# A streaming encoder step on one core: GpSimd's two-tensor operations issued as pieces of at most 256 columns

## The chip, the core and the metric

The kernel runs on one core of a Trainium2 chip. The metric is the device time of one execution in microseconds (us); the time of a kernel is the median of several executions. Five engines take part: TensorE (PE in the profile; PEld are its weight loads), VectorE (DVE), ScalarE (ACT), GpSimd (POOL), and SyncE (SP), which issues the DMAs.

## What is computed

One inference step of a one-layer encoder, for 512 prompt frames with 16 meta tokens ahead of them (T columns) and 32 frames of a running stream. All arrays are float32.

```
x <- x + 1/2 * SwiGLU_1(RMSNorm(x))
h  = RMSNorm(x);  z = h @ W_in_all        # conv B, C, v | q latent | kv latent | rotary key | two gates
conv = W_conv_out(B * dwconv3_causal(C * v))
mla  = W_mla_out(chunk-causal latent attention, 16 heads, QK RMS norm)
x <- x + W_out_all(sigmoid(gate_conv) * conv + sigmoid(gate_mla) * mla)
x <- x + 1/2 * SwiGLU_2(RMSNorm(x))
```

The outputs are x of both groups and the caches for conv, kv latents and rotary keys. The model width is 1024, the FFN width 2816.

## The kernel before

Activations lie transposed: 128 features on the partitions, tokens on the columns (T = 560, or L = 544 without the meta tokens). To keep float32 precision, each operand of a matmul is held as two parts: `hi`, a cast by ScalarE, and `lo`, what the cast lost, a subtraction on VectorE or GpSimd. Each product is three matmuls (`mm3`, L136 to L139): hi*hi, hi*lo, lo*hi. The program is:

1. **First FFN** (`ffn`, L175). The gate and up projections go in pairs of column blocks, with a Strassen-like scheme on VectorE (`operands`, `combine`); the down projection follows in groups (`down`). At the end of each up job `up_job.finish` (L370) writes u into the pair `ah`/`al`; `al` is subtracted on GpSimd. As `down` ends, `done` (L613) calls `gained` (L476) per block of 128 features: GpSimd squares y (L484, L486) and adds it to the sum `sq` (L487); `token_rstd` (L489) then sums `sq` over the features on TensorE (L494).
2. **Mix stretch** (L655 on). Attention, head by head, is written in order, with `fill(us)` calls between its parts; `fill` (L881) draws from `stream` (L849), which has 48 blocks of plain projection matmuls (the conv, gate and conv-out columns, tile `f`). The next block's weights are loaded by `block` (L857) with `E=GP`, so their `lo` part `wl` is made by GpSimd. GpSimd also makes the conv taps' sums `cv` (L825), the products `b1` (L835, L836), and the squares `sqk` (L914) and `sqw` (L948) for the norms of K and Q. VectorE carries the norms' small chains (`rsqrt`, L144), K (L921, L925), Q (L959) and the softmax scaling `pw` (L1110).
3. **Merge.** For each of 8 blocks m, `gate` (L1204) loads a gate column block `sg`, multiplies it by R2 on GpSimd (L1207) and applies the sigmoid on ScalarE; `cb` is multiplied by it (L1217, GpSimd); after the `w_mla_out` product VectorE multiplies `sg` by it (L1220), GpSimd adds `cb` (L1221), and `split` (L1222) makes `mh`/`ml`. The `w_out_all` product of block m = 0 needs `mh` of all 8 blocks, in order of k.
4. **Second FFN**, as the first, and the output.

The subtraction's engine is chosen in `split`:

```
def split(hi, lo, src, E=None):
    a = S.copy(hi, src)
    return a, (E or V).tensor_sub(lo, src, f(hi))
...
block = lambda u: load([u[0]], E=GP)
...
split(ah[:, j], al[:, j], u[j], GP)
```

Weights arrive by SP's DMAs in `load` (L94): raw tile `wr` (2 buffers), `wh` and `wl` (3 buffers each). A framework draws the dependences from the columns that each instruction reads and writes, sets the semaphores, and orders each engine's instructions at build time with a model of their durations; on the chip each engine works its list in that fixed order.

Of the kernel before, what the change touches and what calls it, by code (L numbers as in the profile page):

```python
# [50 lines left out]
WMAX = KD * P  # L51


@with_exitstack
def encoder_step(ctx: ExitStack, tc: tile.TileContext, i, o):
    nc = tc.nc
    V, S, PE, GP = nc.vector, nc.scalar, nc.tensor, nc.gpsimd

    def dma(out, in_):
        return nc.sync.dma_start(out, in_)  # L60
# [454 lines left out]
    with ExitStack() as es:  # L515
# [15 lines left out]
        with tc.tile_pool(name="ps0", bufs=4, space=PSUM, reuse_waits="tile") as psum:  # L531
# [43 lines left out]
            for t, step in enumerate((3, 5, 8, 10, 6)):  # L575
                junk = pool.tile([P, D], F32, tag="tg", name="junk", bufs=2)
                src = xp[:, t] if t < 4 else xm[:MS]
                n = P if t < 4 else MS
# [54 lines left out]
        for ts in ((0, 1), (2, 3), (4,)):  # L633
            ps = acc()
            for k0, k1 in ((0, KD - 1), (KD - 1, KD)):
                for t in ts:
                    n = P if t < 4 else MS
# [6 lines left out]
            for t in ts:  # L644
                n = P if t < 4 else MS
# [9 lines left out]
    with ExitStack() as es:  # L655
# [423 lines left out]
        for h in range(HEADS):  # L1079
# [24 lines left out]
            n = NV[3] // 2  # L1104
# [36 lines left out]
            for j in range(NQ):  # L1141
                ps = bank("t")
                for t in range(j, NQ):
                    a = PO[t] + META + j * P
# [154 lines left out]
def build(inputs):  # L1299
    nc = bacc.Bacc("TRN2", target_bir_lowering=False, num_devices=1, dynamic_dma_scratch_size=1024)  # L1300
    arrays, ins = {}, {}
    for name, a in list(inputs.items()) + list(constants().items()):
        a = np.ascontiguousarray(a)
        arrays[f"in_{name}_dram"] = a
        ap = nc.dram_tensor(
            f"in_{name}_dram", a.shape, mybir.dt.from_np(a.dtype), kind="ExternalInput"
        ).ap()
        ins[name] = ap
    outs = [
        nc.dram_tensor(f"out_{n}_dram", s, F32, kind="ExternalOutput").ap()  # L1310
        for n, s in enumerate(_OUTS)
    ]
    with tile.TileContext(nc, schedule_with_timeline_sim=True) as tc:
        encoder_step(tc, ins, outs)
    return nc, arrays
# [6 lines left out]
```

## Time and profile before

| | |
|---|---|
| median of 3 executions | 1459.97 us (1458.66 to 1461.28) |
| profiled execution | 1461.02 us, its span 1459.1 us |
| TensorE busy | 1399.1 us (96%) |
| VectorE busy | 1055.0 us (72%) |
| ScalarE busy | 652.4 us (45%) |
| GpSimd busy | 381.8 us (26%), 283 instructions |
| mean granted TensorE clock | 0.989 of full speed |

Busy time is the time in which an engine had an instruction under way; matmuls overlap, so a busy TensorE may still be slowed. A line number such as L92 is that of the kernel before, and a helper's line stands for all its callers; the names behind it (`out<-in`) say which. FFN 1 ends near 416 us, the mix stretch lies between 432 and 956, the merge between 956 and 1064, FFN 2 after it.

### The profile page before, as it was taken

How to read it: one execution, taken by the hardware profiler on the slowest of the kernel's cores; microseconds unless marked ns; L12 is line 12 of the kernel's file. 1: busy time of each engine (PE TensorE's matmuls, PEld its weight loads, DVE VectorE, ACT ScalarE, POOL GpSimd, SP SyncE). 2: the span in 40 equal slices, each digit the busy share in tenths (PEclk: the TensorE clock that was granted, in tenths of full speed). 3: DMA queues.
4: the chain of work that ended last, by engine and by line, in shares of the span. 5: the costliest groups of instructions: out<-in, count | busy, mean ns of one | idle time of the engine just before them, and what ended most of it. 6: DMA issues, size and time to landing. Idle time of an engine off the chain costs nothing.

```text
span 1459.1 us, 26175 instructions
## 1 busy us (share of the span) xinstructions
PE 1399.1 (96%) x10667; PEld 1361.9 (93%) x10667; DVE 1055.0 (72%) x1703; ACT 652.4 (45%) x1220; POOL 381.8 (26%) x283
## 2 busy tenths in 40 slices
PE   6999999999999999899999999998989999999998
PEld 5899999999899998898899988998989999999998
DVE  5887878787676766966955958545797787978754
ACT  6543443435324354454554555543254353435341
POOL 0000001101474644444423322168410010001010
PEclk9999999999999999999999999998999999999999
DMA  6242323323343321222332224365433233324213
GB/s 169 65 126 71 116 73 102 91 84 87 90 119 90 97 73 57 79 63 60 102 90 78 82 90 151 117 190 158 133 92 97 73 116 88 115 60 130 70 44 94
DMA packets 215630, 141.59 MB, mean 97 GB/s; under 512 B 6415, under 2 KB 202914, under 8 KB 215510
## 3 DMA queue, kind: packets, MB, share of 16 engines
q1 hardware_dynamic: 215510, 139.93, 32.7%
q8 instruction: 83, 1.36, 0.4%
q14 instruction: 37, 0.30, 0.1%
HBM read 124.15 MB, written 15.76 MB: 96 GB/s over the span
## 4 chain that ended last, share of the span: by engine, by line
PE 75%; DVE 12%; issue 5%; POOL 4%; DMA 3%; ACT 2%; SPq 0%; DVEq 0%; POOLq 0%; ACTq 0%
PE b L137 9%; PE b L138 9%; PE b L139 9%; PE acc L137 7%; PE acc L138 7%; PE acc L139 7%; PE f L137 5%; PE f L138 4%; PE f L139 4%; DMA wr<-in_ffn_w_gate_dram 1%; POOL sg L1207 1%; PE late L137 1%; PE late L138 1%; PE late L139 1%; DVE pw L1110 1%
## 5 line engine op out<-in xcount | busy, mean ns | idle before, releaser
L91 ACT CAST wh<-wr 128x1024 fp32r<-128x1024 f32 (+2 forms) x165 | 166.7, 1018 | 238.6 <-PE acc L138 122.3
L137 PE MATMUL f<-xh,wh 128*128 128x272 f32 (+1 forms) x816 | 240.8, 295 | 4.2 <-DVE ext L815 2.1
L138 PE MATMUL f<-xl,wh 128*128 128x272 f32 (+1 forms) x816 | 239.6, 294 | 0.4 <-DVE xl L92 0.2
L139 PE MATMUL f<-xh,wl 128*128 128x272 f32 (+1 forms) x816 | 239.2, 293 | 0.0
L92 POOL TENSOR_TENSOR al<-tu,ah 128x560 fp32r<-128x560 f32 (+1 forms) x40 | 64.3, 1611 | 654.9 <-issue 392.2
L138 PE MATMUL acc<-al,wh 128*128 128x280 f32 (+1 forms) x704 | 203.8, 291 | 3.0 <-POOL al L92 3.0
L137 PE MATMUL acc<-ah,wh 128*128 128x280 f32 (+1 forms) x704 | 202.8, 291 | 1.7 <-ACT ah L91 1.0
L139 PE MATMUL acc<-ah,wl 128*128 128x280 f32 (+1 forms) x704 | 202.9, 291 | 0.0
L92 POOL TENSOR_TENSOR wl<-wr,wh 128x1024 fp32r<-128x1024 f32 (+1 forms) x50 | 119.9, 2399 | 211.2 <-ACT wh L91 191.4
L92 DVE TENSOR_TENSOR wl<-wr,wh 128x1024 fp32r<-128x1024 f32 (+2 forms) x115 | 153.2, 1338 | 24.1 <-ACT wh L91 20.3
L137 PEld LDWEIGHTS f<-xh,wh 128*128 128x128 f32 x816 | 155.2, 190 | 6.1 <-issue 2.3
L138 PEld LDWEIGHTS f<-xl,wh 128*128 128x128 f32 x816 | 155.5, 191 | 1.5 <-DVE xl L92 1.0
L139 PEld LDWEIGHTS f<-xh,wl 128*128 128x128 f32 x816 | 155.2, 190 | 0.3
L137 PE MATMUL b<-xsh,yh 128*128 128x280 f32 (+1 forms) x480 | 139.1, 290 | 0.8 <-ACT kept L319 0.6
L138 PE MATMUL b<-xsl,yh 128*128 128x280 f32 (+1 forms) x480 | 139.0, 290 | 0.0
L139 PE MATMUL b<-xsh,yl 128*128 128x280 f32 (+1 forms) x480 | 138.9, 289 | 0.1
L138 PEld LDWEIGHTS acc<-al,wh 128*128 128x128 f32 x704 | 132.5, 188 | 3.5 <-POOL al L92 3.5
L137 PEld LDWEIGHTS acc<-ah,wh 128*128 128x128 f32 x704 | 131.8, 188 | 2.7 <-ACT ah L91 1.4
L139 PEld LDWEIGHTS acc<-ah,wl 128*128 128x128 f32 x704 | 132.0, 188 | 0.2 <-DVE wl L92 0.2
L91 ACT CAST yh<-ws 128x1024 fp32r<-128x1024 f32 x80 | 84.0, 1049 | 90.1 <-PE b L138 82.3
L92 DVE TENSOR_TENSOR yl<-ws,yh 128x1024 fp32r<-128x1024 f32 x80 | 97.5, 1218 | 32.7 <-ACT yh L91 32.1
L407 DVE SCALAR_TENSOR_TENSOR tu<-acc,R 128x560 f32<-128x560 f32 (+1 forms) x80 | 58.1, 728 | 50.9 <-PE acc L139 50.8
(359 smaller groups left out, 3873.9 us busy)
## 6 DMA issues: line engine op xcount, KB each, us to landing
wr<-in_w_in_all_dram SPq DMA_DIRECT2D x43, 512.0 KB, 4.0
wr<-in_ffn_w_down_dram SPq DMA_DIRECT2D x32, 512.0 KB, 4.2
wr<-in_ffn_w_gate_dram SPq DMA_DIRECT2D x23, 512.0 KB, 3.9
wr<-in_ffn_w_up_dram SPq DMA_DIRECT2D x23, 512.0 KB, 5.1
wq<-in_ffn_w_gate_dram SPq DMA_DIRECT2D x20, 512.0 KB, 4.2
wq<-in_ffn_w_up_dram SPq DMA_DIRECT2D x20, 512.0 KB, 4.2
wr<-in_ffn_w_down_dram SPq DMA_DIRECT2D x16, 384.0 KB, 3.5
gt_dram<-b SPq DMA_DIRECT2D x16, 272.0 KB, 2.1
```

The lines of the kernel that those rows point to most:

```text
L91: a = S.copy(hi, src)
L92: return a, (E or V).tensor_sub(lo, src, f(hi))
L137: PE.matmul(out, a[0], b[0], start=start, stop=False, skip_group_check=onto)
L138: PE.matmul(out, a[0], b[1], start=False, stop=False, skip_group_check=onto)
L139: PE.matmul(out, a[1], b[0], start=False, stop=stop, skip_group_check=onto)
L407: V.scalar_tensor_tensor(t, ps[:, :, :n], 0.5, Rv, op0=ALU.mult, op1=ALU.mult)
L1110: V.tensor_scalar_mul(pv(t), pv(t), inv[:, t : t + 1])
L1207: GP.tensor_mul(sg, sg, R2[:, META:])
```

## The change

`GP`, which was `nc.gpsimd`, becomes a wrapper around it. Calls of tensor_add, tensor_sub and tensor_mul through it are cut along the first free dimension into equal pieces of at most 256 columns, each an instruction of its own; all other operations pass through. `make_identity` and the DMAs are not touched.

```
+class Pieces:
+    def __init__(self, engine):
+        self.engine = engine
+
+    def __getattr__(self, name):
+        op = getattr(self.engine, name)
+        if name not in ("tensor_add", "tensor_sub", "tensor_mul"):
+            return op
+
+        def pieces(out, a, b):
+            n = out.shape[1]
+            step = max(1, 256 // int(np.prod(out.shape[2:])))
+            count = -(-n // step)
+            cuts = [n * j // count for j in range(count + 1)]
+            for lo, hi in zip(cuts, cuts[1:]):
+                last = op(out[:, lo:hi], a[:, lo:hi], b[:, lo:hi])
+            return last
+
+        return pieces
...
-    V, S, PE, GP = nc.vector, nc.scalar, nc.tensor, nc.gpsimd
+    V, S, PE, GP = nc.vector, nc.scalar, nc.tensor, Pieces(nc.gpsimd)
```

## Rows read from the trace of the kernel before

**Rows 1.** The page, busy us (share of the span) and instructions of each engine.

```profile
PE 1399.1 (96%) x10667; PEld 1361.9 (93%) x10667; DVE 1055.0 (72%) x1703; ACT 652.4 (45%) x1220; POOL 381.8 (26%) x283
```

**Rows 2.** Table of stretches: length, busy (count) by engine, PEclk, DMA share, GB/s.

```profile
core 0: us, PE busy (x) PEld busy (x) DVE busy (x) ACT busy (x) POOL busy (x), PEclk, DMA share, GB/s
432.00:956.00 524.00, 503.91 (x3806) 478.79 (x3804) 362.49 (x790) 259.04 (x641) 198.80 (x144) 0.99 0.30 87
...
712.00:722.00 10.00, 7.52 (x48) 7.25 (x47) 9.87 (x18) 3.48 (x12) 5.22 (x5) 0.83 0.30 79
...
1006.00:1012.00 6.00, 4.64 (x37) 4.42 (x36) 2.95 (x3) 2.40 (x4) 6.00 (x5) 1.00 0.63 185
1012.00:1018.00 6.00, 2.58 (x10) 2.06 (x10) 3.21 (x4) 2.74 (x4) 5.12 (x3) 0.66 0.19 55
```

**Rows 3.** TensorE's waits: what waited, for what, total us, times, longest us.

```profile
PE acc L974 <- DVE K L925: 6.2, 5, 2.2
...
PE late L137 <- ACT mh L91: 4.0, 2, 2.0
PE t L1145 <- DVE pw L1110: 3.7, 3, 2.5
PE acc L137 <- DVE Vl L92: 3.7, 3, 2.5
...
PE acc L138 <- POOL al L92: 3.0, 2, 1.5
...
PE f L137 <- DVE ext L815: 2.1, 1, 2.1
```

**Rows 4.** Timeline near 613 and 840 us: start us, us, engine, line.

```profile
613.16 2.48 POOL L92 TENSOR_TENSOR wl<-wr,wh 128x1024 fp32r<-128x1024 f32 x1 [4.15 <-ACT wh L91]
613.33 2.79 DVE L925 TENSOR_TENSOR K<-kpe,rk 128x448 f32<-128x448 f32 x1
...
616.18 0.64 PE L974 MATMUL acc<-ident,K 128*96 128x128 f32 x4 [1.51 <-DVE K L925]
...
840.40 0.62 DVE L925 TENSOR_TENSOR K<-kpe,rk 128x448 f32<-128x448 f32 x1
```

**Rows 5.** Timeline of GpSimd, three instructions one behind the other.

```profile
481.80 0.24 POOL L835 TENSOR_TENSOR b<-b,cv 128x32 f32<-128x32 f32 x1
482.00 1.29 POOL L836 TENSOR_TENSOR b<-b,cv 128x512 f32<-128x512 f32 x1
483.25 2.38 POOL L92 TENSOR_TENSOR wl<-wr,wh 128x1024 fp32r<-128x1024 f32 x1
```

**Rows 6.** Timeline, Q on VectorE and TensorE's wait behind it.

```profile
710.39 4.30 DVE L959 TENSOR_TENSOR Q<-Q,rr 128x1920 f32<-128x1920 f32 x1
...
715.78 0.39 PE L137 MATMUL acc<-wkh,kvh 128*128 128x256 f32 x1 [2.48 <-DVE Vl L92]
```

**Rows 7.** Timeline near 472 us, small VectorE instructions beside GpSimd's.

```profile
471.77 2.31 DVE L153 TENSOR_TENSOR kaa<-rk 128x14 f32<-128x14 f32 x1
...
474.01 1.37 POOL L825 TENSOR_TENSOR cv<-cv,c 128x546 f32<-128x546 f32 x1
...
474.11 1.29 DVE L154 SCALAR_TENSOR_TENSOR kab<-kaa,vk 128x14 f32<-128x14 f32 x1
```

**Rows 8.** Groups by line, GpSimd in the merge: count | busy us, mean ns | idle before.

```profile
L1207 POOL TENSOR_TENSOR sg<-sg,R 128x544 f32<-128x544 f32 x16 | 26.1, 1640 | 31.7 <-DMA sg<-gt_dram 31.7
L1221 POOL TENSOR_TENSOR sg<-sg,cb 128x544 f32<-128x544 f32 x8 | 14.7, 1832 | 0.1
L1217 POOL TENSOR_TENSOR cb<-cb,sg 128x544 f32<-128x544 f32 x8 | 13.8, 1730 | 0.8 <-ACT sg L1208 0.8
```

**Rows 9.** Timeline of GpSimd in the merge: the first and the last of 32.

```profile
961.59 1.36 POOL L1207 TENSOR_TENSOR sg<-sg,R 128x544 f32<-128x544 f32 x1 [30.44 <-DMA sg<-gt_dram]
...
1015.00 2.20 POOL L1221 TENSOR_TENSOR sg<-sg,cb 128x544 f32<-128x544 f32 x1
```

**Rows 10.** Timeline after the first FFN: last sum of squares, TensorE's sums over it.

```profile
422.64 1.37 POOL L487 TENSOR_TENSOR sq<-sq,sqt 128x560 f32<-128x560 f32 x1
...
426.46 1.05 PE L494 MATMUL acc<-ones,sq 128*128 128x1 f32 x8
```

## The prediction

> **What bounds the kernel now.** I read the busy times first, then the table of stretches, then TensorE's own waits, then the spots of the timeline where those waits arise. TensorE is busy for 96% of the span, GpSimd for 26% [rows 1]: a change to GpSimd's instructions can win only where TensorE stands still, and lose only where it is made to. In the mix stretch TensorE is idle for 524.00 - 503.91 = 20.1 us, and between 1006 and 1018 us for (6.00 - 4.64) + (6.00 - 2.58) = 4.8 us [rows 2]. In the list of waits, the mix stretch's idle time ends mostly on VectorE: on K 6.2, on pw 3.7, on Vl 3.7 and on ext 2.1 us, 15.7 us together. That of 1006 to 1018 ends on mh (4.0), and on al TensorE waits 3.0 us [rows 3].
>
> The timeline says why VectorE is late. K at L925 (128x448) took 2.79 us at 613.33, beside a GpSimd subtraction of 1024 columns that ran from 613.16 for 2.48 us; the same instruction took 0.62 us at 840.40, with GpSimd idle. TensorE's wait of 1.51 us ended with it [rows 4]. So VectorE stands until the GpSimd instruction ends. Shorter GpSimd instructions would free it sooner; this is what the change can win.
>
> **The change, part by part.** GpSimd's additions, subtractions and products become pieces of at most 256 columns: the 48 wl of 1024 columns four each, al, sg, cb, cv, sq (544 to 560 columns) three each, sqk four, sqw eight, the 512-column ones two. Counted over all calls this adds 448 instructions to 283 [rows 1].
>
> *Price of a piece.* GpSimd runs one instruction behind the other, so I take the distance between starts, not the recorded lengths. 32 columns occupy 482.00 - 481.80 = 0.20 us, 512 columns 483.25 - 482.00 = 1.25 us [rows 5]: (1.25 - 0.20) / 480 = 2.19 ns a column, and 0.20 - 0.07 = 0.13 us for each instruction. Hence 448 x 0.13 = 58 us of GpSimd time more; a piece of 256 columns takes 0.69 us, one of 181 0.53. Bounds of the price: 0 if the next piece is got ready wholly behind the last, and 0.24 - 0.07 = 0.17 if the recorded length of the 32-column one counts. I take 0.13, since unhindered pieces would follow each other as those rows do. The Trainium skill, GPSIMD Engine Reference, section 3.1, gives 4497 ns for 2048 columns and 2.6 cycles an element at 1.2 GHz; my estimate from these two is 0.06 us an instruction, less than half of the rows' value, and with it the gate stage below would grow by 64 x 0.06 = 3.8 us.
>
> *Mix stretch: gain.* Two patterns have to be told apart. In the first, one VectorE instruction that TensorE waits for meets one long GpSimd instruction: K above, and Q at 710.39, which took 4.30 us and put off the Vl that TensorE waited 2.48 us for at 715.78 [rows 4, 6]. With pieces it stands for the rest of one piece, at most 0.7 us, then runs. In the second, a chain of small VectorE instructions meets it: kaa took 2.31 us behind wl, and when the next GpSimd instruction began at 474.01 the next small one, kab, took 1.29 [rows 7]. GpSimd and VectorE alternate, so a chain of four small instructions would stand behind each of wl's four pieces and win nothing. By this I take of K's 6.2 us 4.5, of pw's 3.7 2.3, of Vl's 3.7 2.4 and of ext's 2.1 (behind such a chain) 0.3: 9.5 us. A quarter of it I let go to the wait that is next, on ScalarE's casts and on the chain of small instructions: 7.2. Two smaller terms: sqk's pieces need only the part of K already copied, which shortens the road to K (0.8); and the clock, granted at 0.83 between 712 and 722 us after the 2.48 us wait [rows 2], need not fall there: 0.17 x 10 = 1.7, of which I take 1.0. Sum: 9.0 us gained, between 4 (patterns judged too kindly) and 12.
>
> The 48 wl are 0.4 to 0.5 us later; TensorE never waits for one now, only for al [rows 3], so the depth of three weight buffers covers that. SP's next load into wr waits for wl's last piece and starts as much later; it has two buffers and the same cover.
>
> *Gate stage (L1207, L1217, L1221): cost.* Here GpSimd works without a pause: 26.1 + 14.7 + 13.8 = 54.6 us of instructions in the 55.6 us from 961.59 to 1015.00 + 2.20 = 1017.20 [rows 8, 9], and its last sum, the one at 1015.00, releases the last mh that TensorE waits for [rows 3, 9]. Its 32 instructions become 96; 64 x 0.13 = 8.3 us (0 to 10.9 by the bounds). VectorE's work in between still stands in GpSimd's way as before. What may cover it is TensorE's work on the next block of output columns, if the order drawn up at build time puts it ahead of the wait: between 1006 and 1018 us 37 + 10 matmuls ran [rows 2], where the first seven k-steps of the first block have 42, so a few of the next block already stood there. Six k-steps of it, 36 matmuls at 4.64 / 37 = 0.125 us, would be 4.5 us. I take them as covered: 8.3 - 4.5 = 3.8, and 0.7 for the clock, which is at 0.66 there already [rows 2] and may stay low longer. Cost 4.5 us, between 0 and 12.6.
>
> *End of the first FFN: cost.* The squares of eight blocks (L484 to L487) run on GpSimd without a pause until 422.64 + 1.37 = 424.0; TensorE's sum over them starts at 426.46 [rows 10]. 8 blocks x 2 instructions x 2 pieces x 0.13 = 4.2 us later is 428.2: 1.7 us late. Its first matmuls read only the first pieces' columns; I take 1.0 (0 to 1.7).
>
> *The tails of the two FFNs.* Each ends on al twice (1.5 us of the 3.0 in each) [rows 3]. Four pieces more at 0.13 are 0.5, but the first half of the columns is there after two of three pieces: 0.3 for both, between -0.5 and 1.0. The other 36 al, the start's two wl, RR and sqq stand under TensorE's matmuls: nothing; without this cover an al would cost 0.26.
>
> Sum: -9.0 + 4.5 + 1.0 + 0.3 = -3.2 us. The profiled execution took 1461.02 us (span 1459.1), 1.05 above the median of the three runs: 1457.8 against it, **1456.8** against the median.
>
> **The rivals.** *Slower: the gate stage is GpSimd's alone.* Each piece costs its recorded 0.17, nothing of the next block is put ahead, and the clock stays down for another 3.4 us at half: 10.9 + 1.7 instead of 4.5, so -9.0 + 12.6 + 1.3 = +4.9, 1464.9 us. It decides once what stays uncovered there passes 9.0 - 1.3 + 2.9 = 10.6 us. For it speaks that GpSimd has no pause in the stage [rows 8, 9]; against it the spacing [rows 5] and the five matmuls already moved ahead.
>
> *Alternation eats the gain.* The Trainium skill, SBUF — State Buffer, section "Who interferes with whom", says that whoever issues first holds the pair that the two engines share for the whole instruction and the other fully blocks. The rows behave so [rows 7]; as a mechanism here: if VectorE's long instructions also come in runs, as pw's four and Q's products do, each stands behind a piece in turn. The mix stretch then gives 3 instead of 9.0: -3 + 4.5 + 1.3 = +2.8, 1462.8 us. Against it speaks K, a single instruction [rows 4].
>
> *The gate stage is fully covered.* The new order fills the wait with the next two blocks: -9.0 + 0 + 0.5 = -8.5, 1451.5 us. For it speaks that the builder sees the longer GpSimd chain when it orders TensorE; against it, that it placed the last two k-steps so early that TensorE waited for both (two waits, 4.0 us [rows 3]).
>
> That the change does nothing can be ruled out: the calls in question go through GP or through split's E=GP, and both are the wrapper.
>
> **How the numbers follow.** Chances: forecast 0.42, gate stage uncovered 0.23, alternation 0.14, fully covered 0.21. A measurement here can tell 0.2%, 2.9 us, from no change. The forecast sits at that edge: I give just over half of it to faster, most of the rest to no change; the fully covered case is faster; the two others are divided between same and slower. Faster 0.44, same 0.29, slower 0.27. The range: from 1449 (fully covered, mix gain near its bound of 12) to 1466 (uncovered, mix gain near 8); below and above I leave about 2 in 10.
>
> **What would show it.** Right: VectorE's K L925 never above 1.4 us, TensorE's waits on K, pw and Vl together down from 13.6 to some 5 us, GpSimd's count at 731 and its busy time near 440 us, the last mh some 8 us later after the gate stage's start, TensorE's wait for mh grown by some 4. Wrong: VectorE's small instructions each lengthened by half a microsecond with K no earlier; mh no later; a wait on wl, which I hold covered; or TensorE's instructions in another order through the mix stretch, with waits that this trace doesn't have.

## The result and the profile after

The changed kernel takes 1446.41 us (median of 4 runs, 1444.58 to 1451.63), the kernel before 1460.03 beside it: a ratio of 0.9909, 95% interval 0.9896 to 0.9923, so 13.6 us or 0.9% faster. The prediction had the direction, but 1456.8 us, and its range began at 1449.

The profiled execution took 1446.04 us (span 1444.1), against 1461.02 before. The page's busy times answer to [rows 1]:

```profile
PE 1394.5 (97%) x10667; PEld 1360.9 (94%) x10667; DVE 1001.0 (69%) x1703; ACT 652.3 (45%) x1220; POOL 492.8 (34%) x731
```

GpSimd has its 448 instructions more. VectorE, of which the change says nothing, is busy for 54.0 us less with the same 1,703 instructions: this is time in which it used to stand still within an instruction. Its busy time counts that.

To see where the 15 us went I cut both executions at the same four places: the first matmul of the query latents, the merge's first on vh, its first on mh, its last on mh. The table of stretches of the kernel before:

```profile
core 0: us, PE busy (x) PEld busy (x) DVE busy (x) ACT busy (x) POOL busy (x), PEclk, DMA share, GB/s
427.62:956.53 528.91, 508.64 (x3843) 483.40 (x3841) 366.31 (x802) 259.66 (x642) 200.28 (x146) 0.99 0.30 87
956.53:1005.94 49.41, 49.41 (x386) 49.41 (x386) 24.87 (x22) 19.95 (x27) 42.32 (x26) 0.97 0.66 199
1005.94:1063.68 57.74, 52.96 (x388) 52.21 (x387) 37.70 (x28) 17.12 (x22) 32.13 (x20) 0.91 0.43 123
1063.68:1459.00 395.32, 379.22 (x2989) 375.93 (x2987) 299.57 (x407) 165.68 (x242) 35.53 (x22) 0.99 0.31 89
```

and of the changed one:

```profile
428.47:942.11 513.64, 505.00 (x3843) 483.28 (x3841) 337.19 (x802) 259.79 (x642) 246.62 (x393) 0.99 0.30 90
942.11:991.59 49.48, 49.48 (x387) 49.48 (x386) 18.83 (x21) 18.85 (x26) 44.48 (x68) 0.97 0.62 190
991.59:1048.01 56.42, 51.01 (x388) 50.79 (x387) 29.13 (x29) 18.27 (x24) 47.46 (x68) 0.94 0.46 136
1048.01:1444.00 395.99, 379.46 (x2989) 376.16 (x2987) 294.16 (x407) 165.76 (x242) 57.10 (x66) 0.99 0.30 89
```

Up to the query latents +0.85 us, the mix stretch -15.3, the merge's first projection +0.1, its second -1.3, the second FFN +0.7. TensorE's idle time in the mix stretch fell from 20.3 to 8.6 us; the other 3.6 us there are busy time of the same 3,843 matmuls. They belong to the same stops. The busy time of the weight loads (PEld) is the same in both tables, 483.40 and 483.28 us, so the loads stand still for 15.1 us less, nearly the whole 15.3. In the count of busy time a matmul that begins only after the one ahead of it has ended counts in full, and one that overlaps with it only in part: the traces have 27 of the first kind in this stretch before and 11 after, and what they add beyond the usual share of their form is 6.5 and 2.4 us. The clock has no part in it: by the trace TensorE was granted 1.2 instead of 2.4 GHz for 7.5 us of this stretch before and for 7.3 after.

TensorE's waits in the mix stretch, 428 to 942 us (waiting line, what it waited for, total us, times, longest), answer to [rows 3]:

```profile
PE acc L997 <- DVE K L948: 4.1, 2, 2.7
PE t L1184 <- ACT pM L1178: 1.5, 1, 1.5
PE f L160 <- DVE ext L838: 1.2, 1, 1.2
PE acc L160 <- DVE Vl L115: 0.6, 1, 0.6
```

pw is gone, Vl nearly. K's line never reaches the 2.79 us of [rows 4] again; its durations (shortest, median, longest, in ns) in the view of that line:

```profile
L948 DVE TENSOR_TENSOR K<-kpe,rk x8: 618/878/1169, 473.2 to 883.4; 128x448 f32<-128x448 f32 x8
```

Counted over the whole mix stretch of both traces, 35 VectorE instructions of the kernel before took over 0.9 us longer than the shortest of their form, 14 of them over 2 us longer, all beside a GpSimd instruction; afterwards there is one. What [rows 7] showed for kaa and kab is what went.

The second projection of the merge holds one wait now, in the list of waits from 942 to 1048 us; before, it was 4.0 us on mh (twice) and 0.8 on ml:

```profile
PE late L160 <- ACT mh L114: 5.4, 1, 5.4
```

**One more thing differs.** The instructions of TensorE, VectorE, ScalarE and SyncE are the same, but the build's scheduler put them in another order: set side by side, the two traces differ in 201 places on TensorE, 135 on VectorE and 98 on ScalarE. So two causes have to be told apart: the pieces themselves, and the order that came with them.

### The profile page after: what moved, and what is told of

Same layout as the page of the kernel before. It is cut to its first block, busy times and chain, and to the rows that moved or that the text cites. A ratio compares the mean times of both kernels' runs of the same rounds, so it can differ in the third digit from the quotient of the medians.

```text
span 1444.1 us, 26675 instructions
## 1 busy us (share of the span) xinstructions
PE 1394.5 (97%) x10667; PEld 1360.9 (94%) x10667; DVE 1001.0 (69%) x1703; ACT 652.3 (45%) x1220; POOL 492.8 (34%) x731
## 4 chain that ended last, share of the span: by engine, by line
PE 79%; POOL 7%; DVE 6%; issue 4%; DMA 2%; ACT 1%; SPq 0%; POOLq 0%; ACTq 0%; DVEq 0%
PE b L160 9%; PE b L161 9%; PE b L162 9%; PE acc L160 7%; PE acc L161 7%; PE acc L162 7%; PE f L160 6%; PE f L161 6%; PE f L162 6%; POOL sg L71 2%; POOL sq L71 1%; PE t L160 1%; PE t L1168 1%; POOL cb L71 1%; PE late L160 1%
## 5 line engine op out<-in xcount | busy, mean ns | idle before, releaser
L71 POOL TENSOR_TENSOR al<-tu,ah 128x187 fp32r<-128x187 f32 (+3 forms) x120 | 106.5, 919 | 612.7 <-issue 374.5
L71 POOL TENSOR_TENSOR wl<-wr,wh 128x256 fp32r<-128x256 f32 x196 | 151.9, 804 | 150.0 <-ACT wh L114 131.1
L115 DVE TENSOR_TENSOR wl<-wr,wh 128x1024 fp32r<-128x1024 f32 (+2 forms) x115 | 141.4, 1236 | 37.4 <-ACT wh L114 32.9
L115 DVE TENSOR_TENSOR yl<-ws,yh 128x1024 fp32r<-128x1024 f32 x80 | 103.4, 1293 | 38.0 <-ACT yh L114 37.7
L161 PE MATMUL b<-xl,wh 128*128 128x280 f32 (+1 forms) x320 | 92.5, 289 | 0.0
```

The source lines that it names most:

```text
L71: last = op(out[:, lo:hi], a[:, lo:hi], b[:, lo:hi])
L161: PE.matmul(out, a[0], b[1], start=False, stop=False, skip_group_check=onto)
```

## The experiments

Theory A (the prediction's): small VectorE instructions stand for less time behind a GpSimd instruction, so the gain is the pieces' in whatever order. Theory B: the gain is the new order's. To separate them, some kernels below keep a given order. A first build reads off each engine's sequence, a second one chains each engine's instructions in it, without adding a wait on a semaphore; GpSimd's order is left to the scheduler, and in the built programs it differs in places from kernel to kernel; what that is worth was not tested.

```diff
+    for e, ranks in MODE["order"].items():
...
+        for a, b in zip(ranks, ranks[1:]):
+            tc.add_manual_dep(now[e][b], now[e][a].name, NOSYNC, reason="order")
```

"Old order" is that of the kernel before, "new order" that of the changed one. Which of GpSimd's operations are cut is chosen by the wrapper: **w** the low halves of the streamed weights, **g** the three lines of the gate stage, **r** the rest (FFN, squares, convolution); in the code g is the site "m". The table has all runs but e11, a single execution that is told below. Each ratio is against executions of the kernel before that were timed beside that kernel. The lengths are from tables of stretches as above, so each is that of one profiled execution; here the mix stretch is counted from the stream's first matmul to the merge's first, "idle" is TensorE's in it, and the last column is the second projection.

| kernel | cut | order | median us | ratio [95%] | mix us | idle us | 2nd projection us |
|---|---|---|---|---|---|---|---|
| before | - | old | 1461.2 | 1 | 506.4 | 19.4 | 57.7 |
| e2 | - | new | 1459.0 | 0.9977 [0.9964, 0.9991] | 510.7 | 22.0 | 49.4 |
| e1 | w g r | old | 1459.2 | 0.9979 [0.9966, 0.9992] | 490.1 | 8.6 | 63.1 |
| changed | w g r | new | 1446.4 | 0.9909 [0.9896, 0.9923] | 490.8 | 8.6 | 56.4 |
| e5 | w | old | 1450.9 | 0.9932 [0.9917, 0.9947] | 496.2 | 13.0 | 58.0 |
| e3 | w | new | 1439.9 | 0.9855 [0.9838, 0.9872] | 491.4 | 9.4 | 49.2 |
| e6 | g | old | 1473.4 | 1.0080 [1.0066, 1.0094] | 506.3 | 20.4 | 66.2 |
| e7 | w r | new | 1440.2 | 0.9853 [0.9839, 0.9867] | 490.8 | 8.7 | 48.5 |
| e8 | r | new | 1449.6 | 0.9920 [0.9907, 0.9933] | 500.1 | 16.1 | 49.4 |
| e4 | w r | free | 1447.4 | 0.9900 [0.9885, 0.9916] | 490.7 | 8.7 | 57.7 |
| e12 | w | free | 1450.9 | 0.9928 [0.9915, 0.9940] | 497.2 | 12.9 | 55.7 |
| e10 | w, 512 columns | new | 1447.4 | 0.9911 [0.9896, 0.9927] | 501.1 | 15.6 | 48.5 |
| e9 | w, 128 columns | new | 1440.4 | 0.9855 [0.9842, 0.9869] | 492.5 | 10.2 | 48.6 |

### Pieces or order: e1 and e2

e1 is the changed kernel with the old order, e2 the kernel before with the new one. Of e1's edit, the lines that choose the two builds (in e2 `False` and `True` are exchanged):

```diff
+    MODE.update(pieces=False, order=None)
+    nc, _ = build_one(inputs)
...
+    MODE.update(pieces=True, order=order)
+    return build_one(inputs)
```

> The change did two things: it cut GpSimd's operations on two tensors into pieces, and the order in which the scheduler puts the instructions of the other engines came out differently. Here GpSimd's operations are in pieces, while TensorE, VectorE, ScalarE and SyncE have the order of the kernel before, instruction by instruction. Theory of the sharing (small VectorE instructions no longer stand still behind a long GpSimd one): the whole gain stays, 1444 to 1450 us, and TensorE's idle time between the latent projections and the gate stage falls from 20.3 us to about 9. Theory of the order (the gain is the schedule's): no gain, 1459 to 1464 us, idle time there still about 20 us.

> The other half: GpSimd's operations whole as before, the other four engines in the order of the changed kernel. Theory of the sharing: 1457 to 1463 us, VectorE's added time over its shortest in the mix stretch back from 48 to about 72 us. Theory of the order: 1444 to 1449 us with VectorE's time still long. If both halves give a part, each of the two runs lies between, and the two gains add up to about 13.6 us.

Neither theory's time came: each half gives 2 us by the medians, some 3 by the ratios, both together 13.6. The stretches say why; those of e1 are of its fastest execution, 7 us below its median (e11 takes this up). In the mix stretch theory A holds: the pieces make it 16.3 us shorter in the old order (506.4 to 490.1), and the new order alone makes it 4.3 longer. TensorE's idle time in e1 is 8.6 us, as that theory had it. The second projection goes the other way: the new order alone makes it 8.3 us shorter (57.7 to 49.4), the pieces 5.4 longer (57.7 to 63.1). The changed kernel takes the gain of each and pays for the pieces in the second projection.

### What the gate stage's pieces cost: e4, e6, e7

e4 and e7 leave the gate stage whole and cut everything else; e4 leaves the order to the scheduler, e7 keeps the new one. e6 cuts the gate stage alone, in the old order.

```diff
-            GP.tensor_mul(cb, cb, sc)
+            GPM.tensor_mul(cb, cb, sc)
...
-            GP.tensor_add(sg, sg, cb)
+            GPM.tensor_add(sg, sg, cb)
```

> Pieces everywhere but in the gate stage (gates, products and sums of the merge are whole), scheduler free. By the prediction's sum the pieces there cost 4.5 us, so this would give 1442 us. By the two traces, where the stretch of the merge got no longer (57.5 to 56.2 us) though GpSimd's part of it went from 55.6 to 62.6 us, it gives nothing: 1445 to 1448 us.

> The order of the changed kernel, pieces everywhere but in the gate stage. Differs from the changed kernel in the gate stage alone, and from the run with only the weights cut in every other place. If the pieces of the gate stage are the whole of what that run gained over the changed kernel: 1439 to 1441 us. If the pieces elsewhere (feed-forward, squares, convolution sums) cost time: 1441 to 1445 us.

> The order of the kernel before, and pieces only in the gate stage. The prediction's sum puts 4.5 us on this: 1464 to 1467 us, with the matmuls of the second projection taking 61 to 63 us from first to last instead of 57.5. If that stage has slack: 1460 to 1462 us.

e4 came out as its second reading had it (1447.4 us) and would have settled the matter wrongly: the pieces in the gate stage would seem free. e7 shows otherwise. It has the same instructions as e4, and its second projection takes 48.5 us instead of 57.7; the run is at 1440.2 us, by the first of its readings. The table of that stretch, of e4:

```profile
990.80:1048.52 57.72, 53.18 (x388) 52.33 (x387) 30.23 (x28) 17.13 (x22) 39.30 (x46) 0.91 0.43 124
```

and of e7:

```profile
993.34:1041.87 48.53, 48.53 (x388) 48.53 (x387) 28.66 (x27) 16.71 (x22) 39.27 (x45) 1.00 0.49 142
```

e4 waits 3.9 us on mh and 0.6 on ml, and its granted clock is 0.91; e7 doesn't wait at all, at 1.00. The difference is where TensorE's matmuls on the late parts of mh stand. Read off the two programs, so many matmuls of this projection stand ahead of the first that reads a part:

```
part of mh (k-step)          5    6    7
before, e4, e12             30   36   45
changed, e7 (new order)     34   62  103
```

In the new order the second and the third block of output columns are begun before the first is finished. With the gate stage whole the free scheduler gives the old arrangement, matmul for matmul (e4, e12), with the gate stage cut the new one: so it is the cut of that stage that turned the order, and the order that hid it. At the 0.125 us of a matmul, 103 - 45 = 58 matmuls are 7.2 us of cover ahead of part 7. Ahead of part 5 only 4 were added (34 against 30), and it is there, after 34 matmuls, that the changed kernel has its one wait of 5.4 us.

Against e7 the pieces of the gate stage cost the changed kernel 1446.4 - 1440.2 = 6.2 us by the medians. By the ratios it is 0.56%, 8 us, and by the second projection 56.4 - 48.5 = 7.9: so 6 to 8 us. Each was timed beside runs of the kernel before, and the ratios' intervals don't touch. In the old order (e6) they cost 12 us, more than either reading; more on that below.

### Which pieces make the gain: e3, e5, e8

```diff
-            block = lambda u: load([u[0]], E=GP)
+            block = lambda u: load([u[0]], E=GPW)
```

> The order of the changed kernel, with pieces only in the low halves of the streamed weights (4 pieces of 256 columns for a block of 1024 instead of 2 of 512), and every other GpSimd operation whole. If the length of the weights' instructions beside the small VectorE chains is what counted: 1446 to 1450 us. If what counted are the squares of K and Q, which VectorE's chain waits for and which are whole here: 1454 to 1460 us. If the order alone did it: 1444 to 1449 us, as in the run with all whole.

> The order of the kernel before on the four engines, and only the low halves of the streamed weights in pieces. The runs with one half of the change each gained 2 us, both together 13.6: the first traces say that pieces shorten the mix stretch under either order (506.4 to 490.1 us under the old one) and lengthen the gate stage (57.5 to 62.9 us). If these parts simply add: 1443 to 1448 us, with a gate stage as before (57 to 58 us). If the old order can't use shorter weight instructions (the medians of the run with all pieces, 1459 us, against its profiled execution of 1452.5): 1455 to 1460 us.

> The order of the changed kernel, pieces everywhere but in the streamed weights and the gate stage. If the weights alone make the gain in the mix stretch: 1456 to 1460 us, as with all whole in this order. If squares of K and Q in pieces help by releasing the chain: 1450 to 1455 us.

(The aside in the first is wrong: a block's low half is one instruction of 1,024 columns in the kernel before, not two of 512.) In the new order the weights alone bring the mix stretch from 510.7 to 491.4 us, and cutting the rest too adds only 0.6. Without them the rest brings it to 500.1 (e8, 1449.6 us, at the edge of its second reading): the two overlap, probably because a chain freed at one instruction may then meet the next; no run tests that. In the old order the weights give 10.2 us (506.4 to 496.2) and the rest 6.1 more. e5 fell between its two expectations: its second projection is as before, its mix stretch isn't down to 490. e3 expected 1446 to 1450 and gave 1439.9, because I hadn't yet seen that leaving the gate stage whole wins there as well. Which operations of the rest help in e8, the squares or the convolution's sums, was not separated.

### The length of a piece: e9, e10

The line of e10's edit that sets the length; e9 has `step=128`, and e3, from which both differ in this alone, 256. The first text is e10's, the second e9's, and "the same" in the first means the second's kernel:

```diff
+    MODE.update(sites="w", step=512, order=order)
```

> The same with pieces of 512 columns, 2 for a block. If the length of one instruction is what counts: between whole (1459.0 us) and 256 (1439.9 us), about half way, 1445 to 1452 us. If any cut does, because VectorE gets its turn at each boundary: 1439 to 1442 us.

> As the run with only the weights cut (order of the changed kernel, all else whole), with pieces of 128 columns: 8 instead of 4 for a block. If the time that a small VectorE instruction stands behind one GpSimd instruction is what counts, shorter pieces give a little more: 1436 to 1440 us. If each piece costs GpSimd some 0.13 us that now matters (160 pieces more, 21 us of GpSimd's time, its weights late for TensorE): 1441 to 1446 us.

With the order fixed and only the weights cut, the mix stretch is 510.7 us at 1,024 columns, 501.1 at 512, 491.4 at 256 and 492.5 at 128. Half the length gives half the gain, so it is the length of one instruction that counts, and not that there is a boundary at all. At 128 nothing is left to win (1440.4 us, between e9's two readings), and the added instructions (192 more than in e3, not the 160 of the expectation) cost nothing that can be seen: GpSimd is busy for 246.92 of 492.46 us there.

### All else free: e12

> Only the streamed weights in pieces and the scheduler free. It then puts TensorE's matmuls of the second projection in the order of the kernel before. If the mix stretch takes its gain from the shorter weight instructions and the second projection its time from the order: a mix stretch of 490 to 497 us, a second projection of 57 to 58 us, in all 1446 to 1452 us. If the pieces alone carry the gain of the run with only the weights cut: 1439 to 1442 us.

This is e3 with the scheduler free (no diff beyond that). 497.2 us of mix stretch, 55.7 of second projection, 1450.9 in all: near the first reading, and far from the second. The pieces don't carry e3's time without the order.

### The spread of e1: e11

The eleven other runs of e1 took 1455.1 to 1460.9 us, the profiled one 1452.5. e11 is e1 again.

> A second look at all pieces in the old order, whose runs spread from 1452.5 to 1460.9 us around 1459 while the profiled one was the fastest. If the usual run loses its 7 us in the gate stage: the second projection takes 66 us or more from first to last instead of 62.9, as with pieces in that stage alone. If it loses them in the mix stretch: that takes 495 to 498 us instead of 490.1.

1465.14 us, slower than any of e1's twelve, with a mix stretch of 490.7 and a second projection of 69.5 us. Against e1's profiled execution the span is 12.9 us longer: 8.8 of that lie in the merge (its two projections take 52.1 and 69.5 us instead of 49.7 and 63.1), most of the rest ahead of the mix stretch and behind the merge. So the greater part of the loss is in the gate stage, and the first reading was right; but its cause was none that I had listed. In VectorE's timeline of e11 (start us, us, engine, line):

```profile
974.96 7.45 DVE L118 TENSOR_TENSOR wl<-wr,wh 128x1024 fp32r<-128x1024 f32 x1 [0.22 <-ACT wh L117]
...
995.27 8.93 DVE L118 TENSOR_TENSOR wl<-wr,wh 128x1024 fp32r<-128x1024 f32 x1 [0.21 <-ACT wh L117]
```

beside the second of these, GpSimd's in the same execution:

```profile
995.15 1.65 POOL L74 TENSOR_TENSOR cb<-cb,sg 128x181 f32<-128x181 f32 x3
...
1001.46 1.66 POOL L74 TENSOR_TENSOR cb<-cb,sg 128x181 f32<-128x181 f32 x3
```

and TensorE's:

```profile
1004.26 0.59 PE L165 MATMUL late<-mh,wl 128*128 128x272 f32 x1 [8.45 <-DVE wl L118]
```

A subtraction that takes 1.21 us a little later took 8.93: it began at 995.27, and ended 1.08 us after the last of 15 GpSimd pieces (five rows of three, the first and the last shown, from 995.15 to 1001.46 + 1.66 = 1003.12). It was not let in between any two of them, and TensorE waited 8.45 us for it. In e1's profiled execution the same instruction got in after the first of three pieces, which took 3.12 us then instead of 1.66:

```profile
988.18 3.12 POOL L74 TENSOR_TENSOR cb<-cb,sg 128x181 f32<-128x181 f32 x3
988.28 1.57 DVE L118 TENSOR_TENSOR wl<-wr,wh 128x1024 fp32r<-128x1024 f32 x1 [0.22 <-ACT wh L117]
```

In e6 the long standing happened too:

```profile
973.14 9.06 DVE L119 TENSOR_TENSOR wl<-wr,wh 128x1024 fp32r<-128x1024 f32 x1 [0.22 <-ACT wh L118]
```

with GpSimd's pieces back to back up to 979.48 + 1.64 = 981.12, 15 again, counted from the one that ran at 973.14:

```profile
979.48 1.64 POOL L74 TENSOR_TENSOR cb<-cb,sg 128x181 f32<-128x181 f32 x3
```

In e6 the merge takes 4.9 us longer than in e1's profiled execution (51.5 + 66.2 against 49.7 + 63.1), with waits of TensorE on wh (2.0 us) and wl (1.1) in it that the latter doesn't have. So this is likely a part of e6's 12 us, and likely what e1 loses in its usual run; neither is shown, since no usual run of e1 was profiled. In the kernel before, the gate stage's longest such case stood behind one GpSimd instruction only: 2.38 us at 979.07, 1.17 above the shortest.

## Why the prediction was right or wrong

Two terms failed, both towards a longer time: the gain in the mix stretch was put too small, and the gate stage was put at a cost where it came out at a gain.

**Mix stretch: the mechanism right, the term too small.** -9.0 us predicted, -15.3 measured. The waits themselves were read well: K, pw and Vl together were to fall from 13.6 to some 5 us, and are 4.7 (4.1, none and 0.6). The failing step is the one after: a quarter of the gain was given away to waits that would come next. They hardly came (pM's wait grew from 0.5 to 1.5 us): idle time fell by 11.7 us in all, more than the 9.5 before that discount, because waits too small for my list went too (sqq 0.9 us, and several of 0.2 to 0.5). The other 3.6 us, in TensorE's busy time, are what restarting after those stops had cost, which I had put at nothing. The clock's 1.0 didn't come: the low clock at 712 to 722 us went, but another came at 663 to 670 (0.76). No run tests the 0.8 for sqk by itself. K's line stayed at 1.17 us or less, as said (1.4).

**Alternation.** This rival is refuted for the mix stretch. The chains of small instructions do meet piece after piece: from the stream's first matmul to the merge's first, 72 VectorE instructions are over 0.3 us longer than the shortest of their form, against 46 before. But what each stands is mostly the rest of one piece of 0.7 us instead of up to 2.4.

**Price of a piece: right for pieces that follow each other, too low where VectorE works beside them.** A piece of 181 columns was to take 0.53 us. In e11 five rows of three such pieces start from 995.15 to 1001.46: 6.31 / 12 = 0.53. The gate stage's GpSimd work, 55.6 us by [rows 9], now runs from 947.11 to 1008.03 + 1.64 = 1009.67, 62.6 us: +7.0 for the 8.3 predicted. The changed kernel's timeline of GpSimd there, the first and the last row:

```profile
947.11 5.31 POOL L71 TENSOR_TENSOR sg<-sg,R 128x181 f32<-128x181 f32 x8 [32.66 <-DMA sg<-gt_dram]
...
1008.03 1.64 POOL L71 TENSOR_TENSOR sg<-sg,cb 128x181 f32<-128x181 f32 x3
```

The sign of a busy time near 440 us failed: it is 492.8, 111.0 more than before, or 0.25 us for each of the 448 instructions instead of 0.13. A part is that the recorded lengths of pieces overlap (0.57 us at a spacing of 0.53). By the instruction the FFNs pay most: the al rows of the list of groups come to 108.7 us after and 64.3 before, 0.55 us for each of 80 instructions more. e1's rows above show pieces made to wait by a VectorE instruction between them; that it is the same with al is likely, and not shown. It cost next to no time, since these pieces stand under TensorE's matmuls.

**Gate stage: the price about right, the cover wrong.** +4.5 us predicted for the second projection, -1.3 measured. With the order held, the pieces cost 6 to 8 us (e7) and 5.4 (e1's profiled execution), somewhat more than the forecast's 4.5. What failed is the step that counted 36 matmuls, 4.5 us, as moved ahead of the wait: in the old order there are none more than before, in the new one 58, and they also hid what the kernel before had been losing there, 4.0 us of waits and a clock at 0.91. That the builder might do this stood among the rivals as "fully covered" with 0.21, at 1451.5 us; it is the case that came, joined to a mix gain beyond the 12 that I allowed. The sign that I gave for it, TensorE's order, was named for the mix stretch alone. The wait for mh grew from 4.0 to 5.4, not by 4.

**The rest.** The end of the first FFN was to cost 1.0 us: from the key-value projection's first matmul to the query latents it is 13.36 us instead of 12.25, so 1.1. The tails of the FFNs (+0.3) are within the 0.7 us by which the last stretch differs; nothing separates them. "A wait on wl, which I hold covered" did not come in the changed kernel's profile, but did in e11 (8.45 us), on a wl that VectorE makes.

**A version that beats both.** e3, e7 and e9 agree: 1439.9 to 1440.4 us, 1.45% below the kernel before and some 6 us below the changed one. The weights cut to 256 columns, the gate stage whole, TensorE and the rest in the new order.

## What to carry to other kernels

As here, cut one engine's instructions where another engine's chain of small ones stands behind them, and leave them whole where they are themselves the chain that the next stage waits for. When a scheduler orders the program, a change of one engine's instructions may reorder all the others: hold the order fixed in an experiment before any part of a gain is put down to the instructions, and hold the order that suits the chain, as a kernel may keep it without the pieces that brought it about.

## What was unexpected of the hardware

The kernel before showed a VectorE instruction standing behind one GpSimd instruction at a time. With pieces back to back it stood three times through a whole run: 8.93 us (e11) and 9.06 us (e6), behind 15 pieces each, and 7.45 us, at 974.96 in e11. In the changed kernel's mix stretch there is one such case, through the four pieces of a block (e4 and e7 have it too, 2.18 and 2.17 us), VectorE's row and GpSimd's:

```profile
484.62 2.17 DVE L975 SCALAR_TENSOR_TENSOR vq<-vq,rq 128x20 f32<-128x20 f32 x1
```

```profile
483.95 2.81 POOL L71 TENSOR_TENSOR wl<-wr,wh 128x256 fp32r<-128x256 f32 x4
```

At other places VectorE got in after the rest of one piece (1.57 us in e1). What decides between the two stays open; both were seen in one kernel, e1 and e11. The Trainium skill, SBUF — State Buffer, section "Who interferes with whom", says that whoever issues first gets the pair of ports shared by the two for the whole instruction and that the other is fully blocked; it says so of VectorE's modes that use both ports, and of an instruction with two inputs in SBUF, as all of these are, that it contends with GpSimd's reads. The rows of whole instructions agree with a full block (2.38 us for 1.21). Those of e6 and e11 go further, as here VectorE was blocked for a run of instructions, and the measurement decides.
